# The second attention of a two-layer decoder: values as the stationary operand in two column halves, the weights divided ahead of their transposes, the mask added by transfers

## The chip, the cores and the metric

The kernel runs on one core of a Trainium2 chip. The core has five engines that each work through an instruction stream of their own: TensorE (PE, matmuls and transposes), VectorE (DVE), ScalarE (ACT), GpSimd (POOL, which here adds a few tiles and issues transfers) and SyncE (SP, which issues most transfers). The metric is the time of one execution on the device in microseconds. The kernel before was run three times: 976.5, 976.67 and 976.83 us, median 976.67.

## The reference, cut to what matters

One sequence of 256 tokens with 1024 features goes through two layers. The first has a differential attention, the second a forgetting attention whose keys, values and forget gates are computed once, between the layers. Only the second attention is changed:

```
def forgetting_attention(h, w_q, w_o, k, v, F):
    q = (h @ w_q).reshape(b, s, B_HEADS, HEAD_DIM)     # 16 heads of 64
    def block(args):                                   # 2 blocks of 128 queries
        causal = q_pos[:, None] >= k_pos[None, :]
        decay = jnp.transpose(Fqb, (0, 2, 1))[..., None] - F_k[:, :, None, :]
        logits = jnp.einsum('bqhd,bkhd->bhqk', qb, k) * scale + decay
        logits = jnp.where(causal, logits, -jnp.inf)
        p = jax.nn.softmax(logits, axis=-1)
        return jnp.einsum('bhqk,bkhd->bqhd', p, v)
    ...
    return o.reshape(b, s, B_WIDTH) @ w_o
```

Around it stand four SwiGLU feed-forward blocks, the first attention, the norms and the modulation by the vector c.

## The kernel before

Everything is held transposed, features on partitions and tokens along the rows, so that 128 features by 256 tokens is one tile. Projections are made of f32 products split in three: a weight piece `raw` is cast to a short part `wh` by ScalarE, VectorE computes the residue `wl`, activations are split into `HH` and `HL` in the same way, and `mm3` issues the three matmuls wh x high, wl x high, wh x low. Each of the three is a 128x128 load and a matmul that moves 256 columns (258 where two more columns carry a shift). The weights stream from HBM by SyncE's transfers through six buffers.

TensorE, ScalarE and VectorE take their instructions in the order in which the program writes them (the class `InOrder` records every call at line 99, which is why nearly all rows of the profile name that line). `InOrder` keeps an estimate of each engine's clock, and casts and residues of coming weight pieces are put into the gaps that this estimate shows (`bg`, `fill_act`, `fill_dve`). What GpSimd issues is not ordered this way; it is ordered by a scheduler as its inputs and buffers come free.

The second attention is `attention_b`. It works on eight pairs of heads, c = 0 to 7, in a pipeline of groups, t = 0 to 10. Between two groups a number of fill steps run on TensorE (`fills`): first the rest of the q projection (tiles `lq`), then the output projection of the finished pairs (`op.steps`, tiles `pw`). The tuple in the last loop gives the number of fill steps ahead of each group. A group t does four things for four pairs:

- pair t, `scores` and `exps`: two heads of 64 features stand on the two row halves of the array, and `sb` gets 128x128 logits for the first block of queries and 128x256 for the second. VectorE subtracts logits and decay and takes the minimum (tile `d`, `nm`), ScalarE exponentiates in place and sums the rows (`sm`). `d` holds 384 columns a head: 128 for the first block, 256 for the second; queries stand on partitions.
- pair t-1, `weights_t` and `weights_out`: three 128x128 transposes a head through the identity in the constants' tile `tri`, into the banks `wa` and `wb`, copied to `wta` by ScalarE and to `wtb` by VectorE.
- pair t-2, `values` and `divide`: three matmuls a head, the transposed weights stationary (128x128), 64 columns of `vb` moving; the result, queries on partitions, lies in the second half of `wb`. VectorE then multiplies it by the reciprocal of the row sums (`rsb`, `onb`).
- pair t-3, `out_t` and `out_split`: two transposes of `onb` into free columns of the score banks `sb`, so that features stand on partitions again; ScalarE casts to `obh`, VectorE computes the residue `obl`, as the output projection needs them.

At the end of a group `masked(t+1)` adds the causal mask on VectorE to the two diagonal 128x128 blocks of each head's `d`, and `decay(t+2)` loads the next decays: one transfer for each head, issued by GpSimd at line 1236 from a small DRAM tile `fdram` that is repeated on all partitions. `d` has six buffers, three pairs; a load therefore waits for the transposes of the pair three before it.

Of the kernel before, what the change touches and what calls it, by code (L numbers as in the profile page):

```python
# [10 lines left out]
F32 = mybir.dt.float32  # L11
# [3 lines left out]
ALU = mybir.AluOpType  # L15
PSUM = bass.MemoryType.PSUM

P = 128
# [3 lines left out]
HD = 64  # L22
# [81 lines left out]
def trunk(ctx, tc, a, out):  # L104
    nc = tc.nc
    InOrder.ready = {}
    pe = InOrder(tc, nc.tensor, 0.0, 1 / 2350)
    act = InOrder(tc, nc.scalar, 0.13, 1 / 1200)
    dve = InOrder(tc, nc.vector, 0.08, 1 / 960)
# [11 lines left out]
    def sbank(name):  # L121
        return pp.tile([P, 512], F32, tag="s", name=name, bufs=2)
# [7 lines left out]
    mm = pe.matmul  # L130
# [776 lines left out]
    for k in range(0, NC, 2):  # L907
# [3 lines left out]
        if k % 4:  # L911
            i = k // 4
# [309 lines left out]
    def attention_b():  # L1222
# [9 lines left out]
        def decay(c):  # L1232

            for hd in (2 * c, 2 * c + 1):
                d = cp_.tile([P, 384], F32, tag=DT[hd % 6], name=f"d{hd}")
                nc.gpsimd.dma_start(d, bass.AP(fdram.tensor, fdram.offset + hd * (P + S), [[0, P], [1, P + S]]))
                ds[hd] = d

        def masked(c):

            m2 = mask.rearrange("p (o k) -> p o k", o=1).to_broadcast([P, 2, P])
            for m in range(2):
                diag = ds[2 * c + m].rearrange("p (b k) -> p b k", k=P)[:, ::2]
                dve.tensor_tensor(diag, diag, m2, op=ALU.add)

        r = late_pairs("wq", q[:2], None, AF.Exp)
        for c in range(2):
# [15 lines left out]
        def exps(c, sb):  # L1263
# [10 lines left out]
                                   bias=nm[:, cc:cc + 1], scale=-1.0, accum_out=sm[:, cc:cc + 1])  # L1274
            sms[c] = sm

        def weights_t(c, ta, tb):
            for j in range(6):
                d, b = ds[2 * c + j // 3], j % 3
                pe.transpose(ta[:, j * P:j * P + P] if j < 4 else tb[:, (j - 4) * P:(j - 3) * P],  # L1280
                             d[:, b * P:b * P + P], ident)

        def weights_out(c, ta, tb):
            w0 = cp_.tile([P, 512], F32, tag="hidh8", name=f"wta{c}")
            w1 = cp_.tile([P, 256], F32, tag="hidh9", name=f"wtb{c}")
            act.copy(w0, ta)
            dve.tensor_copy(w1, tb[:, :256])
            st[c] = [w0[:, j * P:j * P + P] for j in range(4)] + [w1[:, j * P:j * P + P] for j in range(2)]

        def values(c, po):  # L1290

            for m in range(2):
                hd = 2 * c + m
                wt = st[c][3 * m:3 * m + 3]
                vs = slice((hd % 8) * HD, (hd % 8) * HD + HD)
                v0, v1 = vb[0][hd // 8][:, vs], vb[1][hd // 8][:, vs]
                mm(po[:, m * HD:m * HD + HD], wt[0], v0, start=True, stop=True)
                mm(po[:, P + m * HD:P + m * HD + HD], wt[1], v0, start=True, stop=False)
                mm(po[:, P + m * HD:P + m * HD + HD], wt[2], v1, start=False, stop=True)

        def divide(c, po):
            rs = kp.tile([P, 4], F32, tag="rs", name=f"rsb{c}")
            dve.reciprocal(rs, sms[c])
            on = kp.tile([P, 256], F32, tag="w512b", name=f"onb{c}")
            dve.tensor_tensor(on.rearrange("p (g d) -> p g d", g=4), po.rearrange("p (g d) -> p g d", g=4),
                              rs.rearrange("p (g o) -> p g o", o=1).to_broadcast([P, 4, HD]), op=ALU.mult)
            st[c] = on

        def out_t(c, pz):
            for qt in range(2):  # L1310
                pe.transpose(pz[qt], st[c][:, qt * P:qt * P + P], ident)

        def out_split(c, pz):
            oh, ol = o[c]
            for qt in range(2):
                act.copy(oh[:, qt * P:qt * P + P], pz[qt])
            for qt in range(2):
                qs = slice(qt * P, qt * P + P)
                dve.tensor_tensor(ol[:, qs], pz[qt], oh[:, qs].bitcast(F32), op=ALU.subtract)

        def group(t):

            cs, cw, cv, co = (c if 0 <= c < NP else None for c in (t, t - 1, t - 2, t - 3))
            sb = [sbank(f"sb{t}_{m}") for m in range(2)] if cs is not None or co is not None else None
            ta = abank(f"wa{t}") if cw is not None else None
            tb = bbank(f"wb{t}") if cw is not None or cv is not None else None
            if co is not None:
                pz = [sb[m][:, 384:] for m in range(2)]
                out_t(co, pz)
            if cs is not None:  # L1330
                scores(cs, sb)
            if cv is not None:
                values(cv, tb[:, 256:])
            if cw is not None:
                weights_t(cw, ta, tb)
            if co is not None:
                out_split(co, pz)
            if cs is not None:
                exps(cs, sb)
            if cv is not None:  # L1340
                divide(cv, tb[:, 256:])
            if cw is not None:
                weights_out(cw, ta, tb)
            if t + 1 < NP:
                masked(t + 1)
            if t + 2 < NP:
                decay(t + 2)

# [6 lines left out]
                for _ in op.steps():  # L1355
                    yield

        masked(0)
        fill = fills()
        for t, n in enumerate((3, 9, 7, 7, 7, 7, 7, 7, 7, 6, 5)):  # L1360
            for _ in range(n):
                next(fill)
            group(t)
        return op, fill

    pace[0] = PACE[5]
# [133 lines left out]
```

## Time and profile before

| What | Value |
| --- | --- |
| runs of the kernel, median of 3 | 976.67 us |
| span of the profiled execution, first to last instruction | 974.4 us |
| the runs' median above that span | 2.27 us |
| moved from HBM, on average over the span | 274 GB/s |
| second attention, first scores to last output transposes | 728.8 to 778.5 us of the span |
| granted TensorE clock, mean | 0.999 |

The profile is one execution. The page gives its span and no second figure for the whole execution, so what lies around the span is known only as the difference to the runs' median. Times in the views are microseconds from the span's start. TensorE appears as two rows of records, matmuls (PE) and loads of the stationary operand (PEld); an f32 matmul is recorded as two passes, each with a load of its own. Matmuls are pipelined, so their lengths overlap, and what one costs is read from the distance between starts.

### The profile page before, as it was taken

The page shows a single profiled execution, that of the slowest core. Times are in us where ns is not written, and L with a number is a line of the kernel's source. Part 1 is how long each engine was busy: PE and PEld are TensorE (multiplying, and loading weights), DVE is VectorE, ACT ScalarE, POOL GpSimd, SP SyncE. Part 2 cuts the span into 40 slices and gives each one's busy share as a digit, 9 for nine tenths or more (in the row PEclk, how much of TensorE's full clock was granted, in tenths as well). Part 3 has the DMA queues.
Part 4 walks back from the last instruction along what each step waited for, and adds up shares of the span by engine and source line. Part 5 has one row for each costly group of instructions (what it writes and reads, how often), then busy time and mean ns, then how long its engine had stood idle before and what let it go on. Part 6 is the DMA issues. An engine that isn't in the chain of part 4 may idle for free.

```text
span 974.4 us, 20491 instructions
## 1 busy us (share of the span) xinstructions
PE 963.7 (99%) x8124; PEld 939.9 (96%) x8124; DVE 818.5 (84%) x1372; ACT 552.4 (57%) x902; POOL 54.6 (6%) x94
## 2 busy tenths in 40 slices
PE   8999999999999999999999999999999999999997
PEld 6999999998999999999997999999998999999997
DVE  7989979989999999878899989989977699555575
ACT  5466545566787645455576554445567576455432
POOL 0000200000112000000000000000011014300000
PEclk9999999999999999999999999999999999999999
DMA  9988999967776699888959899998885337978651
GB/s 360 415 352 279 332 372 339 345 225 272 293 239 232 209 381 370 293 287 314 329 179 370 308 338 337 345 314 319 297 278 174 104 109 228 266 149 276 185 152 44
DMA packets 69473, 268.22 MB, mean 275 GB/s; under 512 B 9417, under 2 KB 10225, under 8 KB 59266
## 3 DMA queue, kind: packets, MB, share of 16 engines
q1 hardware_dynamic: 66016, 259.69, 76.1%
q0 software_dynamic: 3072, 6.92, 2.5%
q8 instruction: 63, 1.03, 0.4%
q10 hardware_dynamic: 290, 0.32, 0.1%
q14 instruction: 32, 0.26, 0.1%
HBM read 264.75 MB, written 2.66 MB: 274 GB/s over the span
## 4 chain that ended last, share of the span: by engine, by line
PE 97%; DVE 1%; DMA 1%; ACT 0%; issue 0%; SPq 0%; DVEq 0%; ACTq 0%
PE po L99 25%; PE pg L99 21%; PE pu L99 21%; PE pf L99 5%; PE pv L99 5%; PE pw L99 4%; PE lp L99 4%; PE pqk L99 3%; PE wb L99 1%; PE lq L99 1%; PE lu L99 1%; PE lg L99 1%; PE pk L99 1%; PE sb L99 1%; DMA ada<-in_ada 1%; PE s L99 1%
## 5 line engine op out<-in xcount | busy, mean ns | idle before, releaser
L99 ACT CAST wh<-raw 128x1024 fp32r<-128x1024 f32 (+1 forms) x360 | 347.3, 975 | 210.8 <-PE pu L99 82.0
L99 DVE TENSOR_TENSOR wl<-raw,wh 128x1024 fp32r<-128x1024 f32 (+1 forms) x360 | 398.6, 1126 | 70.9 <-ACT sg L99 20.3
L99 DVE CUSTOM_DVE_ANT_0 ada<-ada,cact,vecs 128x1024 f32<-128x1024 f32 x160 | 203.6, 1279 | 0.4 <-DMA ada<-in_ada 0.4
L99 PE MATMUL pg<-HH,wh 128*128 128x256 f32 x608 | 168.0, 276 | 0.0
L99 PE MATMUL pg<-HH,wl 128*128 128x256 f32 x608 | 167.9, 276 | 0.0
L99 PE MATMUL pu<-HH,wh 128*128 128x256 f32 x608 | 167.9, 276 | 0.0
L99 PE MATMUL pu<-HL,wh 128*128 128x256 f32 x608 | 167.9, 276 | 0.0
L99 PE MATMUL pg<-HL,wh 128*128 128x256 f32 x608 | 167.9, 276 | 0.0
L99 PE MATMUL pu<-HH,wl 128*128 128x256 f32 x608 | 167.9, 276 | 0.0
L99 PE MATMUL po<-hidh,wh 128*128 128x256 f32 x528 | 145.7, 276 | 0.0
L99 PE MATMUL po<-hidh,wl 128*128 128x256 f32 x528 | 145.7, 276 | 0.0
L99 PE MATMUL po<-hidl,wh 128*128 128x256 f32 x528 | 145.7, 276 | 0.0
L99 PEld LDWEIGHTS pg<-HH,wh 128*128 128x128 f32 x608 | 114.1, 188 | 0.7 <-issue 0.6
L99 PEld LDWEIGHTS pg<-HH,wl 128*128 128x128 f32 x608 | 114.1, 188 | 0.0
L99 PEld LDWEIGHTS pu<-HH,wh 128*128 128x128 f32 x608 | 114.1, 188 | 0.0
L99 PEld LDWEIGHTS pg<-HL,wh 128*128 128x128 f32 x608 | 114.1, 188 | 0.0
L99 PEld LDWEIGHTS pu<-HL,wh 128*128 128x128 f32 x608 | 114.1, 188 | 0.0
L99 PEld LDWEIGHTS pu<-HH,wl 128*128 128x128 f32 x608 | 114.1, 188 | 0.0
L99 PEld LDWEIGHTS po<-hidh,wh 128*128 128x128 f32 x528 | 99.1, 188 | 0.0
L99 PEld LDWEIGHTS po<-hidl,wh 128*128 128x128 f32 x528 | 99.1, 188 | 0.0
L99 PEld LDWEIGHTS po<-hidh,wl 128*128 128x128 f32 x528 | 99.1, 188 | 0.0
L99 ACT CAST hidh<-hf 128x512 fp32r<-128x512 f32 x44 | 27.3, 621 | 40.5 <-DVE hf L99 40.4
(226 smaller groups left out, 1848.4 us busy)
## 6 DMA issues: line engine op xcount, KB each, us to landing
raw<-in_win SPq DMA_DIRECT2D x176, 512.0 KB, 6.8
ada<-in_ada SPq DMA_DIRECT2D x79, 1024.0 KB, 7.2
raw<-in_wout SPq DMA_DIRECT2D x48, 384.0 KB, 5.3
raw<-in_wout SPq DMA_DIRECT2D x48, 320.0 KB, 5.5
raw<-in_wqk SPq DMA_DIRECT2D x16, 512.0 KB, 5.8
raw<-in_wo SPq DMA_DIRECT2D x16, 512.0 KB, 5.8
raw<-in_wlast SPq DMA_DIRECT2D x16, 512.0 KB, 4.5
raw<-in_wv SPq DMA_DIRECT2D x8, 512.0 KB, 7.2
```

Of the source, the lines that this page charges most:

```text
L99: return self.tc.keep_in_program_order(f(*args, **kw))
```

## The change

Four things change in `attention_b`, and nothing outside it. In `values` the 64 columns of v of one head become the stationary operand and the transposed weights move, 256 columns for the first 128 keys (both blocks of queries) and 128 for the second; the two heads of a pair write partitions 0 to 63 and 64 to 127 of one bank, which puts them on two column halves of the array. The result has features on partitions, so `out_t` is gone, and with it a stage of the pipeline: ten groups instead of eleven. The weights of a head must then lie side by side, so `weights_t` orders its six blocks anew. The division can no longer follow the values; `scale` divides `d` itself, ahead of the transposes, two fill steps before the group. The mask is no longer added by VectorE: each decay load is followed by a second transfer of GpSimd that adds the mask to the two diagonal blocks. `out_split` becomes one cast and one residue of 256 columns. The numbers of fill steps are changed to suit, and the last four run after the last group.

```diff
--- before.py
+++ after.py
@@ -1235,13 +1235,10 @@
                 d = cp_.tile([P, 384], F32, tag=DT[hd % 6], name=f"d{hd}")
                 nc.gpsimd.dma_start(d, bass.AP(fdram.tensor, fdram.offset + hd * (P + S), [[0, P], [1, P + S]]))
                 ds[hd] = d
-
-        def masked(c):
-
             m2 = mask.rearrange("p (o k) -> p o k", o=1).to_broadcast([P, 2, P])
-            for m in range(2):
-                diag = ds[2 * c + m].rearrange("p (b k) -> p b k", k=P)[:, ::2]
-                dve.tensor_tensor(diag, diag, m2, op=ALU.add)
+            for hd in (2 * c, 2 * c + 1):
+                diag = ds[hd].rearrange("p (b k) -> p b k", k=P)[:, ::2]
+                nc.gpsimd.dma_start(diag, m2, accum_op=ALU.add)
 
         r = late_pairs("wq", q[:2], None, AF.Exp)
         for c in range(2):
@@ -1274,75 +1271,58 @@
                                    bias=nm[:, cc:cc + 1], scale=-1.0, accum_out=sm[:, cc:cc + 1])
             sms[c] = sm
 
+        def scale(c):
+
+            rs = kp.tile([P, 4], F32, tag="rs", name=f"rsb{c}")
+            dve.reciprocal(rs, sms[c])
+            for m in range(2):
+                d = ds[2 * c + m]
+                for qt, (c0, w) in enumerate(QT):
+                    dve.tensor_scalar(d[:, c0:c0 + w], d[:, c0:c0 + w], rs[:, 2 * qt + m:2 * qt + m + 1], None,
+                                      op0=ALU.mult)
+
         def weights_t(c, ta, tb):
-            for j in range(6):
-                d, b = ds[2 * c + j // 3], j % 3
-                pe.transpose(ta[:, j * P:j * P + P] if j < 4 else tb[:, (j - 4) * P:(j - 3) * P],
-                             d[:, b * P:b * P + P], ident)
+            for m, b, to, i in ((0, 0, ta, 0), (0, 1, ta, 1), (0, 2, ta, 2), (1, 2, ta, 3), (1, 0, tb, 0), (1, 1, tb, 1)):
+                pe.transpose(to[:, i * P:i * P + P], ds[2 * c + m][:, b * P:b * P + P], ident)
 
         def weights_out(c, ta, tb):
             w0 = cp_.tile([P, 512], F32, tag="hidh8", name=f"wta{c}")
             w1 = cp_.tile([P, 256], F32, tag="hidh9", name=f"wtb{c}")
             act.copy(w0, ta)
             dve.tensor_copy(w1, tb[:, :256])
-            st[c] = [w0[:, j * P:j * P + P] for j in range(4)] + [w1[:, j * P:j * P + P] for j in range(2)]
+            st[c] = ((w0[:, :2 * P], w0[:, 2 * P:3 * P]), (w1, w0[:, 3 * P:]))
 
         def values(c, po):
 
-            for m in range(2):
-                hd = 2 * c + m
-                wt = st[c][3 * m:3 * m + 3]
-                vs = slice((hd % 8) * HD, (hd % 8) * HD + HD)
-                v0, v1 = vb[0][hd // 8][:, vs], vb[1][hd // 8][:, vs]
-                mm(po[:, m * HD:m * HD + HD], wt[0], v0, start=True, stop=True)
-                mm(po[:, P + m * HD:P + m * HD + HD], wt[1], v0, start=True, stop=False)
-                mm(po[:, P + m * HD:P + m * HD + HD], wt[2], v1, start=False, stop=True)
-
-        def divide(c, po):
-            rs = kp.tile([P, 4], F32, tag="rs", name=f"rsb{c}")
-            dve.reciprocal(rs, sms[c])
-            on = kp.tile([P, 256], F32, tag="w512b", name=f"onb{c}")
-            dve.tensor_tensor(on.rearrange("p (g d) -> p g d", g=4), po.rearrange("p (g d) -> p g d", g=4),
-                              rs.rearrange("p (g o) -> p g o", o=1).to_broadcast([P, 4, HD]), op=ALU.mult)
-            st[c] = on
-
-        def out_t(c, pz):
-            for qt in range(2):
-                pe.transpose(pz[qt], st[c][:, qt * P:qt * P + P], ident)
-
-        def out_split(c, pz):
+            for kt in range(2):
+                for m in range(2):
+                    hd = 2 * c + m
+                    v = vb[kt][hd // 8][:, (hd % 8) * HD:(hd % 8) * HD + HD]
+                    mm(po[m * HD:m * HD + HD, kt * P:], v, st[c][m][kt], start=kt == 0, stop=kt == 1)
+
+        def out_split(c, po):
             oh, ol = o[c]
-            for qt in range(2):
-                act.copy(oh[:, qt * P:qt * P + P], pz[qt])
-            for qt in range(2):
-                qs = slice(qt * P, qt * P + P)
-                dve.tensor_tensor(ol[:, qs], pz[qt], oh[:, qs].bitcast(F32), op=ALU.subtract)
+            act.copy(oh, po)
+            dve.tensor_tensor(ol, po, oh.bitcast(F32), op=ALU.subtract)
 
         def group(t):
 
-            cs, cw, cv, co = (c if 0 <= c < NP else None for c in (t, t - 1, t - 2, t - 3))
-            sb = [sbank(f"sb{t}_{m}") for m in range(2)] if cs is not None or co is not None else None
+            cs, cw, cv = (c if 0 <= c < NP else None for c in (t, t - 1, t - 2))
+            sb = [sbank(f"sb{t}_{m}") for m in range(2)] if cs is not None else None
             ta = abank(f"wa{t}") if cw is not None else None
             tb = bbank(f"wb{t}") if cw is not None or cv is not None else None
-            if co is not None:
-                pz = [sb[m][:, 384:] for m in range(2)]
-                out_t(co, pz)
             if cs is not None:
                 scores(cs, sb)
             if cv is not None:
                 values(cv, tb[:, 256:])
             if cw is not None:
                 weights_t(cw, ta, tb)
-            if co is not None:
-                out_split(co, pz)
             if cs is not None:
                 exps(cs, sb)
             if cv is not None:
-                divide(cv, tb[:, 256:])
+                out_split(cv, tb[:, 256:])
             if cw is not None:
                 weights_out(cw, ta, tb)
-            if t + 1 < NP:
-                masked(t + 1)
             if t + 2 < NP:
                 decay(t + 2)
 
@@ -1355,12 +1335,15 @@
                 for _ in op.steps():
                     yield
 
-        masked(0)
         fill = fills()
-        for t, n in enumerate((3, 9, 7, 7, 7, 7, 7, 7, 7, 6, 5)):
-            for _ in range(n):
+        for t, n in enumerate((3, 9, 8, 8, 8, 8, 7, 7, 6, 4)):
+            for i in range(n):
+                if 1 <= t <= NP and i == n - 2:
+                    scale(t - 1)
                 next(fill)
             group(t)
+        for _ in range(4):
+            next(fill)
         return op, fill
 
     pace[0] = PACE[5]
```

The next rows are TensorE's order in one group of the middle of the attention (sb are the score banks, wa and wb the banks of transposed weights, wb also that of the values). Before:

```order
L99 MATMUL sb_0_9700<-tri,onb_9654 128x128
L99 MATMUL sb_1_9701<-tri,onb_9654 128x128
L99 MATMUL sb_0_9700<-kT,q_9238 128x128
L99 MATMUL sb_1_9701<-kT,q_9238 128x128
L99 MATMUL sb_0_9700<-kT,q_9238 128x256
L99 MATMUL sb_1_9701<-kT,q_9238 128x256
L99 MATMUL wb_9703<-vb,wta_9656 128x64 x4
L99 MATMUL wb_9703<-vb,wtb_9657 128x64 x2
L99 MATMUL wa_9702<-tri,d_9503 128x128 x3
L99 MATMUL wa_9702<-tri,d_9505 128x128
L99 MATMUL wb_9703<-tri,d_9505 128x128 x2
```

and now:

```order
L99 MATMUL sb_0_9721<-kT,q_9238 128x128
L99 MATMUL sb_1_9722<-kT,q_9238 128x128
L99 MATMUL sb_0_9721<-kT,q_9238 128x256
L99 MATMUL sb_1_9722<-kT,q_9238 128x256
L99 MATMUL wb_9724<-wta_9668,vb 64x256
L99 MATMUL wb_9724<-wtb_9669,vb 64x256
L99 MATMUL wb_9724<-wta_9668,vb 64x128 x2
L99 MATMUL wa_9723<-tri,d_9509 128x128 x3
L99 MATMUL wa_9723<-tri,d_9511 128x128
L99 MATMUL wb_9724<-tri,d_9511 128x128 x2
```

The two output transposes at the head are gone, and six values matmuls with 64 moving columns have become four with 256 or 128, the heads in turn.

On VectorE, between the copy of one pair's transposed weights (wtb) and the subtractions for the next pair (ISA, reading sb), stood before:

```order
L99 RECIPROCAL rsb_9578<-smb_9428 128x4
L99 TENSOR_TENSOR onb_9580<-wb_9549,rsb_9578 128x256
L99 COPY wtb_9583<-wb_9549 128x256
L99 TENSOR_TENSOR d_9503<-d_9503,tri 128x2x128
L99 TENSOR_TENSOR d_9505<-d_9505,tri 128x2x128
L99 TENSOR_TENSOR wl<-raw,wh 128x1024
L99 TENSOR_TENSOR obl_9232<-sb_0_9616,obh_9228 128x128
L99 TENSOR_TENSOR obl_9232<-sb_1_9617,obh_9228 128x128
L99 ISA d_9503,nmb_9642<-sb_0_9616,d_9503 128x128
```

and now:

```order
L99 TENSOR_TENSOR wl<-raw,wh 128x1024
L99 TENSOR_TENSOR obl_9232<-wb_9559,obh_9228 128x256
L99 COPY wtb_9591<-wb_9559 128x256
L99 TENSOR_TENSOR wl<-raw,wh 128x1024
L99 RECIPROCAL rsb_9626<-smb_9575 128x4
L99 TENSOR_SCALAR d_9439<-d_9439,rsb_9626 128x128
L99 TENSOR_SCALAR d_9439<-d_9439,rsb_9626 128x256
L99 TENSOR_SCALAR d_9441<-d_9441,rsb_9626 128x128
L99 TENSOR_SCALAR d_9441<-d_9441,rsb_9626 128x256
L99 ISA d_9509,nmb_9656<-sb_0_9638,d_9509 128x128
```

The masks and the division have left this place, and the scaling of the pair's weights stands behind the residue, the copy and a weight residue, ahead of the next pair's subtractions.

On GpSimd's queue, where before only the decay loads stood (d<-fdram, one for each head, in the order of the heads), the first pairs now have:

```order
L1236 DMA d_9391<-fdram 128x384
L1236 DMA d_9393<-fdram 128x384
L1236 DMA d_9397<-fdram 128x384
L1236 DMA d_9399<-fdram 128x384
L1241 DMA d_9391<-tri 128x2x128
L1241 DMA d_9393<-tri 128x2x128
L1236 DMA d_9439<-fdram 128x384
L1241 DMA d_9397<-tri 128x2x128
L1241 DMA d_9399<-tri 128x2x128
L1236 DMA d_9441<-fdram 128x384
L1241 DMA d_9439<-tri 128x2x128
L1241 DMA d_9441<-tri 128x2x128
```

The adding transfers (d<-tri, line 1241) stand between the loads, each behind the load of the same buffer, which it waits for; a load written behind them waits in the queue as well.

## The prediction

> **What bounds the kernel now.** I read the head of the page first, then its chain of work that ended last, then what TensorE waits for, and last the stretch of the second attention by itself.
>
> ```profile
> span 974.4 us, 20491 instructions
> PE 963.7 (99%) x8124; PEld 939.9 (96%) x8124; DVE 818.5 (84%) x1372; ACT 552.4 (57%) x902; POOL 54.6 (6%) x94
> ...
> PE 97%; DVE 1%; DMA 1%; ACT 0%; issue 0%; SPq 0%; DVEq 0%; ACTq 0%
> ```
>
> TensorE (PE) is 97% of the chain that sets the end. A busy TensorE could still be a waiting one, so the list of its waits over the whole span comes next, and with it the stretch from the first to the last attention group.
>
> ```profile
> PE pf L99 <- ACT HH L99: 1.9, 1, 1.9
> PE warm L99 <- DVE one L99: 1.2, 1, 1.2
> PE pw L99 <- DVE nl L99: 0.8, 2, 0.4
> PE pf L99 <- DVE wl L99: 0.2, 1, 0.2
> ...
> 727.00:779.00 52.00, 52.00 (x448) 48.09 (x447) 37.14 (x133) 34.10 (x109) 5.32 (x10) 1.00 0.45 142
> ```
>
> These four waits sum to 4.1 us; none is in the second attention (pf and warm belong to the start, pw<-nl to the first attention). In the stretch, the columns are PE, PE's loads, DVE, ACT, POOL, clock, DMA share, GB/s: TensorE 52 of 52 us at full clock, VectorE 37.1, ScalarE 34.1, transfers at 0.45. So here a microsecond of TensorE work is a microsecond of kernel, and the others have room.
>
> **What a group costs on TensorE.** One group, by the timeline of TensorE (start, length, tiles, shape, count; f32 matmuls have two records, one for each pass):
>
> ```profile
> 753.57 0.28 PE L99 MATMUL pw<-obh,wl 128*128 128x256 f32 x1
> 753.68 0.28 PE L99 MATMUL pw<-obl,wh 128*128 128x256 f32 x1
> 753.80 0.38 PE L99 MATMUL sb<-tri,onb 128*128 128x128 f32 x2
> 754.11 0.93 PE L99 MATMUL sb<-kT,q 64*128 64x128 f32 x8
> 754.97 1.10 PE L99 MATMUL wb<-vb,wta 128*128 128x64 f32 x8
> 755.91 0.61 PE L99 MATMUL wb<-vb,wtb 128*128 128x64 f32 x4
> 756.35 0.61 PE L99 MATMUL wa<-tri,d 128*128 128x128 f32 x4
> 756.80 0.38 PE L99 MATMUL wb<-tri,d 128*128 128x128 f32 x2
> 756.94 0.36 PE L99 MATMUL pw<-obh,wh 128*128 128x256 f32 x1
> ...
> L99 PE MATMUL sb<-kT,q x64: 272/374/378, 728.8 to 766.1; 64*128 64x128 f32 x32, 64*128 64x256 f32 x32
> ```
>
> Starts count, since lengths overlap. The output transposes (onb) take 753.80 to 754.11, the scores 0.86 us, the values (vb) 754.97 to 756.35 or 1.38 us for 12 passes. A values pass moves only 64 columns but comes every 0.11 to 0.12 us: as long as a pass of 128 transposed columns (wa, 0.45 us for 4), so its 128x128 load is what it pays. The last row gives the speed of moving: the scores' passes last 272 ns at 128 columns and 378 at 256, so 128 f32 columns stream in about 0.106 us and 256 in 0.21. The scores are, for each head, 128 and 256 columns in two passes: 0.64 us a head, 1.28 for two heads after one another. They take 0.86. The two heads stand on two row halves of the array, and the row shows these running at the same time: 0.64 of streaming and 0.22 for entering and leaving the split array.
>
> **The change, part by part.**
>
> *Output transposes, gone.* 16 transposes (8 pairs of two). The nearest place without them is the first group, and one without scores is a late group:
>
> ```profile
> 728.61 0.28 PE L99 MATMUL lq<-HL,wh 128*128 128x258 f32 x1
> 728.82 0.93 PE L99 MATMUL sb<-kT,q 64*128 64x128 f32 x8
> 729.68 0.39 PE L99 MATMUL lq<-HH,wh 128*128 128x258 f32 x1
> ...
> 770.89 0.38 PE L99 MATMUL sb<-tri,onb 128*128 128x128 f32 x2
> 771.11 1.00 PE L99 MATMUL wb<-vb,wta 128*128 128x64 f32 x8
> ...
> 772.39 0.61 PE L99 MATMUL wa<-tri,d 128*128 128x128 f32 x4
> ```
>
> From the last full-array matmul to the scores it is 0.21 us without them and 0.43 with them (753.68 to 754.11): 0.22 a pair; in the late group also 0.22 (770.89 to 771.11). Eight pairs: **1.76 us**.
>
> *Values, turned round.* Now 4 matmuls a pair instead of 6; 64 columns of v are stationary, the weights move: 256 and 128 columns for each head, two passes, the heads on two column halves. Column halves are nowhere in this trace. The streaming is exactly that of the scores, so from below it is 0.64 us (halves side by side, free entry and exit), from above 1.28 plus 0.22, 1.50 (one after the other). I take the scores' 0.86, as the nearest row: same moving sizes, same head pairs, half an array each. Then 1.38 becomes 0.86 in the six groups that have scores just ahead, less about 0.04 for the first transposes' load behind a split array: 6 x 0.48 = 2.88. In the last two groups the old block is 1.28 (771.11 to 772.39); the new one has an entry of its own, 0.21 less an ordinary step of 0.12, so 0.95: 2 x 0.33 = 0.66. Together **3.54 us**.
>
> [...]
>
> *VectorE and ScalarE.* From the groups of the stretch and from the first attention, which has the scaling:
>
> ```profile
> L99 DVE TENSOR_TENSOR wl<-raw,wh 128x1024 fp32r<-128x1024 f32 x9 | 11.0, 1219 | 0.2 <-PE pw L99 0.2
> ...
> L99 DVE TENSOR_TENSOR d<-d,tri 128x256 f32<-128x256 f32 x16 | 6.0, 418 | 0.0
> L99 DVE TENSOR_TENSOR obl<-sb,obh 128x128 fp32r<-128x128 f32 x14 | 3.4, 286 | 7.2 <-ACT obh L99 7.2
> L99 DVE TENSOR_TENSOR onb<-wb,rsb 128x256 f32<-128x256 f32 x8 | 3.4, 425 | 3.4 <-PE wb L99 3.4
> L99 DVE COPY wtb<-wb 128x256 f32<-128x256 f32 x8 | 3.3, 415 | 0.0
> ...
> L99 DVE TENSOR_SCALAR nl<-nl,rs x16: 286/317/351, 222.0 to 287.1; 128x128 f32<-128x128 f32 x8, 128x256 f32<-128x256 f32 x8
> ```
>
> VectorE loses 16 x 0.418 of masks, 8 x 0.425 of division and 16 x 0.286 of residues (14.7 us), and gains 16 x (0.286 + 0.351) of scaling and 8 residues of 256 columns at about 0.42 (13.6 us). Even, 36 us in a stretch of about 47. ScalarE's two casts of a pair become one. None of it is on the path; the cover is TensorE's streaming, and it goes only if the order makes TensorE wait, as follows.
>
> *A new wait: the transposes on the scaling.* Counted from the start of a pair's scores (728.82), VectorE's part of its exponentials starts 1.0 later (first row below) and takes up to 4 x 0.35; ScalarE's ends near 3.2 (four of 0.45, second row). Then come, on VectorE, the residue (0.42), the wtb copy (0.42) and a weight residue (1.22), to 4.4 or so, and the scaling of 2 x 0.64, over near 5.7. The next group's transposes come one period (5.0 us, below) plus scores and values (1.7) later: 6.7. Slack 1.0; I take nothing, and up to 0.3 in a group or two where two weight residues stand ahead. Behind the scaling on VectorE stand the next pair's exponentials, behind the transposes on TensorE the output projection.
>
> *The masks by transfer.* POOL issues them in order: a pair's two decay loads, then, once these have landed, two adding transfers.
>
> ```profile
> L99 DVE CUSTOM_DVE_ANT_0 d<-sb,d x32: 281/356/420, 729.8 to 767.9; 128x128 f32<-128x128 f32 x16, 128x256 f32<-128x256 f32 x16
> ...
> L99 ACT ACTIVATE d<-d,nmb x32: 386/452/503, 730.1 to 768.8; 128x128 f32<-128x128 f32 x16, 128x256 f32<-128x256 f32 x16
> ...
> 748.49 0.93 PE L99 MATMUL sb<-kT,q 64*128 64x128 f32 x8
> ...
> 759.81 0.93 PE L99 MATMUL sb<-kT,q 64*128 64x128 f32 x8
> ...
> 765.50 0.93 PE L99 MATMUL sb<-kT,q 64*128 64x128 f32 x8
> ...
> 711.52 1.90 POOL L1236 DMA_DIRECT2D d<-fdram  x3 [185.25 <-PE po L99]
> ...
> 751.76 1.06 POOL L1236 DMA_DIRECT2D d<-fdram  x2 [4.69 <-ACT d L99]
> ...
> DMA to landing us min/median/max: 3.2/3.6/9.7
> ...
> DMA to landing us min/median/max: 2.1/6.4/8.2
> ...
> 814.00:839.00 25.00, 25.00 (x223) 25.00 (x222) 19.41 (x22) 13.32 (x15) 18.39 (x32) 1.00 0.95 265
> ```
>
> A period is 5.69 us (759.81 to 765.50), then about 5.0. The load for the pair two groups ahead goes out 3.3 us behind the scores (748.49 to 751.76), then about 2.8. To that pair's exponentials are left 2 x 5.0 - 2.8 + 1.0 = 8.2 us, for a load of 3.6 (d<-fdram, first landing row) and an adding transfer. The trace has none that adds; the bounds are 2.1 and 8.2 (second landing row: x<-turned, the only transfer from SBUF to SBUF, at a DMA share of 0.95 by the last row). I take 3.6 to 4, as the loads of this very stretch: no wait up to 4.6, and with the 1.0 of slack nothing lost on TensorE up to 5.6. At 8.2, 2.6 us are lost in each round of three groups (a load waits for the transposes of the pair three before it), and there are two rounds: 5.2 in all. The first pair has more time: with both transfers at their longest, 711.5 + 9.7 + 8.2 is 729.4, just ahead of its exponentials at 729.8.
>
> **The sum.** 1.76 + 3.54 = 5.3 us off TensorE's stream; the span becomes 974.4 - 5.3 = 969.1. The runs' median, 976.67, is 2.27 above the profiled span, and what lies around the span doesn't change: **971.4 us**. After the attention TensorE again waits for nothing, so what is saved stays saved.
>
> **The rivals.**
> 1. *Halves overlap in part.* Loads of one half not hidden behind the other's stream, or a head's two passes kept together so that only every other pass has company. A load in the open costs up to 0.10: the eight wta passes take 0.94 behind the scores and 0.84 (771.11 to 771.95) behind full-array work. Three more of them at 0.05 to 0.10 in 8 pairs: 1.2 to 2.4 us; passes kept together: 0.21 x 8 = 1.7. That is 972.6 to 973.8. Against it: the scores overlap fully in the same form. [...] The trace speaks against it for the whole array: full-array steps of 0.11 to 0.12 (753.57, 753.68) leave no room for a load in the open.
> 2. *The change doesn't do what it says: the column halves run one after the other.* The block grows by 0.64 x 8 = 5.1 us: 976.5, no change. For it: two streams over all 128 rows at once, which the row halves of the scores never need.
> 3. *The adding transfers come late,* 5.6 to 8.2 us: 971.4 to 976.6. For it: 6.4 is the median of x<-turned. Against: transfers are at 0.45 here.
> [...]
>
> **How the numbers follow.** Forecast 60% (its own range 969.6, entry and exit free in all 8 pairs, to 972.4); rival 1 15%, rival 2 13%, rival 3 7%, rival 4 5%. The range 969.6 to 976.5 takes in both ends of the unknown block. 0.2% is 1.95 us, about what a measurement of this kernel can tell from no change: faster is under 974.7, which holds the forecast, rival 1 and most of rival 3 (0.81); rival 2 and the rest of 3 are the same (0.14); rival 4 is slower (0.05).
>
> **What would show it.** [...] A wait of TensorE's wa for VectorE's d, or of VectorE's d<-sb for a transfer, shows the two new waits, and the landing time of d<-tri decides rival 3. The prediction is wrong if the values block isn't like the scores block, or if the saved time reappears as a wait of TensorE behind the attention.

## The result, and the profile after

| Kernel | median of the runs, us | lowest to highest | profiled run: time, span |
| --- | --- | --- | --- |
| before (6 runs beside the changed ones) | 976.75 | 976.50 to 981.08 | 976.67 (median of the first three), 974.4 |
| changed (6 runs) | 983.43 | 981.03 to 988.69 | 983.71, 981.7 |

The changed kernel is slower: ratio 1.0068, interval 1.0044 to 1.0092. Forecast were 971.4 us and a range up to 976.5. Runs of one kernel, of the one before too, scatter upwards by some 4 us or more (its cause, as far as one is seen, is in the last section), so single runs are not compared, and the stretches of a trace are.

The head of the changed kernel's page and its chain of work that ended last, as quoted of before:

```profile
span 981.7 us, 20425 instructions
PE 962.2 (98%) x8076; PEld 933.6 (95%) x8076; DVE 820.0 (84%) x1372; ACT 552.2 (56%) x894; POOL 74.5 (8%) x110
...
PE 91%; DVE 3%; issue 3%; DMA 1%; POOL 1%; ACT 1%; DVEq 0%; POOLq 0%; ACTq 0%
```

TensorE has less to do (962.2 us busy against 963.7) and is 91% of the chain, not 97%: what came instead is waiting. The waits of TensorE and, from the list of VectorE, the one for a transfer (in total, times, longest):

```profile
PE wb L99 <- DVE rsb L99: 3.3, 2, 2.4
PE pw L99 <- DVE lt L99: 1.8, 1, 1.8
PE wa L99 <- DVE d L99: 1.4, 2, 0.9
PE wb L99 <- DVE wtb L99: 1.3, 2, 0.9
PE sb L99 <- DVE nmb L99: 0.8, 1, 0.8
```

```profile
DVE d L99 <- DMA d<-tri: 7.1, 4, 2.9
```

All eight waits lie in the second attention, which had none before: 8.6 us. The rows of TensorE name five tiles of VectorE, and it would be easy to look for the fault there. VectorE's own list gives the source: its part of the exponentials, the subtraction that writes d, waited four times, 7.1 us in all, for the adding transfers (d<-tri). The list puts three more waits of this subtraction (2.2, 0.8 and 0.5 us) down to TensorE, but like the four they end 0.16 us behind the landing of an adding transfer: 10.6 us in all, in every pair from the fourth on. In this trace each adding transfer that came late made VectorE late, and TensorE then met whichever of VectorE's tiles it needed next.

TensorE's timeline (start, length, tiles, shape, count), at an undisturbed group and at the longest wait:

```profile
737.45 0.93 PE L99 MATMUL sb<-kT,q 64*128 64x128 f32 x8
738.30 0.43 PE L99 MATMUL wb<-wta,vb 128*64 128x256 f32 x1
738.31 0.43 PE L99 MATMUL wb<-wtb,vb 128*64 128x256 f32 x1
738.57 0.38 PE L99 MATMUL wb<-wta,vb 128*64 128x256 f32 x1
738.58 0.38 PE L99 MATMUL wb<-wtb,vb 128*64 128x256 f32 x1
738.78 0.39 PE L99 MATMUL wb<-wta,vb 128*64 128x128 f32 x4
739.10 0.66 PE L99 MATMUL wa<-tri,d 128*128 128x128 f32 x4
...
739.73 0.37 PE L99 MATMUL lq<-HH,wh 128*128 128x258 f32 x1
...
775.93 0.28 PE L99 MATMUL pw<-obl,wh 128*128 128x256 f32 x1
778.58 0.45 PE L99 MATMUL wb<-wta,vb 128*64 128x256 f32 x1 [2.37 <-DVE rsb L99]
...
779.89 1.12 PE L99 MATMUL wa<-tri,d 128*128 128x128 f32 x4
...
781.08 0.56 PE L99 MATMUL pw<-obh,wh 128*128 128x256 f32 x1
```

The values block is what the forecast said it would be: passes of the two heads start 0.01 us apart, and from the first to the transposes it is 0.80 us (738.30 to 739.10; forecast 0.86, old block 1.38). The saving is there; it was spent on waiting. Behind the wait of 2.4 us the same block takes 1.31 us (778.58 to 779.89) and the six transposes 1.19 (779.89 to 781.08) where they take 0.63 (739.10 to 739.73). Windows of the changed kernel show why (busy time of PE, PE's loads, DVE, ACT, POOL, then granted clock, DMA share, GB/s):

```profile
748.00:758.00 10.00, 7.89 (x68) 6.29 (x68) 7.06 (x23) 6.23 (x18) 7.00 (x8) 1.00 0.58 111
...
768.00:778.00 10.00, 6.56 (x54) 5.41 (x52) 5.15 (x21) 5.34 (x17) 2.46 (x2) 1.00 0.47 93
778.00:788.00 10.00, 9.42 (x69) 8.50 (x70) 5.84 (x15) 5.47 (x10) 0.00 (x0) 0.83 0.36 109
```

The granted clock falls to 0.83 in the window behind the wait. Compared with the undisturbed group, the values block and the transposes lose about 1.1 us there.

Now GpSimd, which issues the loads (L1236) and the adding transfers (L1241). Its timeline in the changed kernel, brackets: idle before, and for whom:

```profile
741.35 2.14 POOL L1236 DMA_DIRECT2D d<-fdram  x2
748.08 2.46 POOL L1241 DMA_DIRECT2D d<-tri  x2 [4.58 <-DMA d<-fdram]
750.05 1.66 POOL L1236 DMA_DIRECT2D d<-fdram  x2
754.62 2.46 POOL L1241 DMA_DIRECT2D d<-tri  x2 [2.92 <-DMA d<-fdram]
756.11 2.14 POOL L1236 DMA_DIRECT2D d<-fdram  x2
762.87 1.23 POOL L1241 DMA_DIRECT2D d<-tri  x1 [4.61 <-DMA d<-fdram]
...
765.26 1.62 POOL L1236 DMA_DIRECT2D d<-fdram  x2
```

and the view of line 1241 by itself (instructions, idle time before them, landing):

```profile
L1241 POOL DMA_DIRECT2D d<-tri x16: 1172/1228/1723, 716.1 to 771.5; - x16
...
  DMA d<-fdram: 31.3, 11
...
DMA to landing us min/median/max: 3.0/5.4/9.3
```

From one pair's loads to the next pair's is 8.70 us (741.35 to 750.05), 6.06 (750.05 to 756.11) and 9.15 (756.11 to 765.26), though the attention wants a pair about every 5. In each round the queue stands still until the loads have landed (31.3 us in all) and issues two adding transfers, 1.2 us each; only then does it reach the next pair's loads. Their buffers had been free for 4 to 6 us by then: the transposes that free them were followed by TensorE's next work at 745.10, 752.48 and 759.21, and the loads went out at 750.05, 756.11 and 765.26. Three theories follow from this, and the runs below set them apart.

- **A, the order in the queue.** The next loads stand behind adding transfers that wait: a chain of load, landing, add, load that is longer than a group.
- **B, the adding transfers themselves.** They take time of the DMA engines, of the SBUF or of GpSimd's issuing; or (**B'**) load and adding transfer in a row are longer than the 8.2 us that three pairs of buffers leave, whatever the queue.
- **C, the scaling.** Not the masks but the new wait of the transposes on the scaled weights sets the end.

### The profile page after: what moved, and what is told of

Same layout as the page of the kernel before. It is cut to its first block, busy times and chain, and to the rows that moved or that the text cites. A ratio compares the mean times of both kernels' runs of the same rounds, so it can differ in the third digit from the quotient of the medians.

```text
span 981.7 us, 20425 instructions
## 1 busy us (share of the span) xinstructions
PE 962.2 (98%) x8076; PEld 933.6 (95%) x8076; DVE 820.0 (84%) x1372; ACT 552.2 (56%) x894; POOL 74.5 (8%) x110
## 4 chain that ended last, share of the span: by engine, by line
PE 91%; DVE 3%; issue 3%; DMA 1%; POOL 1%; ACT 1%; DVEq 0%; POOLq 0%; ACTq 0%
PE po L99 25%; PE pg L99 21%; PE pu L99 21%; PE pf L99 5%; PE pv L99 5%; PE lp L99 4%; PE pqk L99 3%; PE pw L99 2%; PE pk L99 1%; DVE wl L99 1%; DMA d<-tri 1%; PE lq L99 1%; DVE HL L99 1%; PE s L99 1%; PE lu L99 1%
```

## The experiments

Ratios are to the kernel before, run on the same chip; the experiments ran on three chips, so a difference of two medians is rough. Diffs are against the changed kernel unless the text says otherwise.

**The masks back on VectorE**, all else as changed.

```diff
-                nc.gpsimd.dma_start(diag, m2, accum_op=ALU.add)
+        def masked(c):
...
+                dve.tensor_tensor(diag, diag, m2, op=ALU.add)
```

> The changed kernel with the masks added by VectorE again, where they stood before; values in column halves, scaling ahead of the transposes and all else as changed. Theory A (the loss is the round trip in GpSimd's queue: the loads of a pair stand behind the adding transfers of the pair before, which wait for their own loads to land, about 7 us a pair against a period of 5): 970.5 to 972.5 us, TensorE waits for nothing in the second attention. Theory B (adding transfers are costly in themselves, by their traffic or their issue): the same, 970.5 to 972.5. Theory C (the loss is the new wait of the transposes for the scaling, and the masks only coincide with it): over 976.

Measured 972.09 us (971.77 to 976.53, 11 runs), ratio 0.9944 (0.9924 to 0.9965). The only wait of TensorE in the attention, from its list:

```profile
PE pw L99 <- DVE lt L99: 0.6, 1, 0.6
```

C falls: the transposes never wait for the scaling. The terms for transposes and values come out at the forecast's 971.4 within a microsecond, and the transfers alone cost 983.43 - 972.09 = 11.3 us. The traces agree: from the first scores to the last matmul of the output projection it is 58.0 us in the kernel before (728.8 to 786.8), 64.6 in the changed one (728.9 to 793.5) and 53.2 here (728.7 to 781.9), so the saving is 4.8 us of the 5.3 forecast and the loss 11.4. This version beats both kernels.

**The kernel before, with the adding transfers alone** (diff against before).

```diff
-        def masked(c):
...
-                dve.tensor_tensor(diag, diag, m2, op=ALU.add)
+                nc.gpsimd.dma_start(diag, m2, accum_op=ALU.add)
```

> The kernel before with the one edit that the masks are added by transfers; values, division and groups as before. A: a round of about 7 us a pair against a period of 5.7, so over some six pairs 4 to 9 us slower than before, 980 to 986. B: slower too, by 2 us or more. C: no change, 976 to 977.5.

Measured 983.39 us (981.84 to 989.09, 10 runs), ratio 1.0049 (1.0027 to 1.0071). The transfers harm the old kernel as well, by about half as much: the stretch of the attention is 63.5 us in its trace (729.7 to 793.2), 5.5 more than before. Why half was not tested; its period is longer, 5.7 us. In its list of waits they show up under yet another name, the old kernel's output transposes waiting for the divided values:

```profile
PE sb L99 <- DVE onb L99: 3.1, 2, 1.8
```

**The loads issued by SyncE**, the adding transfers alone on GpSimd.

```diff
-                nc.gpsimd.dma_start(d, bass.AP(fdram.tensor, ...
+                sp.dma_start(d, bass.AP(fdram.tensor, ...
```

> The changed kernel with the decay loads issued by SyncE, so that on GpSimd's queue only the adding transfers stand and no load waits behind them. A: most of the loss goes, 971 to 975. B: the adding transfers stay as slow, 979 or more. C: 980 or more.

Measured 983.77 us (982.5 to 988.3, 10 runs), ratio 1.0055 (1.0032 to 1.0078): a miss for A as it was put. The trace shows that the run asked another question. From SyncE's view of the tile d up to 760 us, and from TensorE's waits:

```profile
L99 SPq DMA_DIRECT2D d<-fdram x12: 319/364/432, 726.9 to 753.3; - x12
```

```profile
PE sb L99 <- DVE nmb L99: 4.6, 1, 4.6
PE pw L99 <- DVE lt L99: 2.9, 1, 2.9
```

SyncE reached the first loads only at 726.9 us, behind its weight pieces, where GpSimd issued them at 711.6; the first pair was late, and the largest wait, 4.6 us, comes from that. The wait of 2.9 us (lt) comes later, at 758, and where it comes from stays open. The run says nothing for or against A.

**Masks on VectorE, and plain transfers of the adding ones' shape into tiles that nobody reads** (diff against the version with the masks on VectorE).

```diff
+                nc.gpsimd.dma_start(spare.rearrange("p (b k) -> p b k", k=P), m2)
```

> Masks on VectorE as in the first run, and beside them GpSimd issues plain transfers of the same shape from the same mask into spare tiles that nobody reads: the traffic and the issue without the wait for the loads and without the adding. A: as the first run, within 1 us of it. B, if it is traffic or issue: 2 us or more above the first run. C: as the first run, whatever that is.

Measured 982.06 us (980.33 to 986.34, 10 runs), ratio 1.0037 (1.0017 to 1.0057). Again the order had shifted: nothing ties these transfers to their pair, and GpSimd's scheduler put all sixteen ahead of the later loads. There is a single wait in the attention:

```profile
PE wa L99 <- DVE d L99: 9.4, 1, 9.4
```

A miss as a test of traffic; as a test of the queue it shows what transfers ahead of a load in GpSimd's queue cost, even if no one needs them. So the same was run in the program's order:

```diff
+                tc.keep_in_program_order(nc.gpsimd.dma_start(spare.rearrange("p (b k) -> p b k", k=P), m2))
```

> The fourth run again with GpSimd's queue in program order (there all spare transfers were moved ahead of the loads and held them up once): masks on VectorE, and behind each pair's two loads two plain transfers of the mask's shape into spare tiles. A and B': as with the masks on VectorE alone, 971.5 to 973. B by traffic or issue: 976 or more.

Measured 972.74 us (971.98 to 973.66, 5 runs), ratio 0.9949 (0.9931 to 0.9966), against 972.09 without the transfers. In this kernel's timeline of GpSimd two plain transfers take 1.42 us to issue:

```profile
736.79 1.42 POOL L1241 DMA_DIRECT2D spare<-tri  x2
```

By these medians the plain transfers' bytes and issuing cost 0.65 us, and TensorE's one wait in this attention is the 0.6 us for lt that the version without them has too. As a stand-in for adding ones they are not complete: the bytes are the same, the packets are not, as GpSimd's queue shows (packets, MB, share of the DMA engines), here and, second, in the changed kernel:

```profile
q0 software_dynamic: 3840, 9.02, 3.2%
```

```profile
q0 software_dynamic: 7424, 9.02, 4.1%
```

With the masks on VectorE the queue has 3072 packets, so the plain transfers make 768 and the adding ones 4352. For bytes B falls here; for packets and for the adding itself it is settled only by the runs below that keep the adding transfers.

**The adding transfers one group behind their loads:** eight buffers, loads three groups ahead, and in the queue, kept in the program's order, the loads of pair t+3 before the adding transfers of pair t+2, which by then find their loads landed.

```diff
+            if t + 3 < NP:
+                decay(t + 3)
             if t + 2 < NP:
-                decay(t + 2)
+                added(t + 2)
```

> The changed kernel with eight buffers for the decays instead of six, the loads three groups ahead, and GpSimd's queue in program order with a pair's adding transfers one group behind its loads: load of pair t+3, then adding for pair t+2. So no adding transfer waits for a fresh load, and each has some 8 us until its use. A (queue order) and B' (load and adding one after the other are longer than the 8 us window): 971 to 974. B (adding transfers cost in themselves): 978 or more.

Measured 975.28 us (971.83 to 983.19, 10 runs), ratio 0.9988 (0.9962 to 1.0014). The profiled run was the lowest, 971.83; in its attention TensorE waits only 0.7 us for lt, and the stretch from the first scores to the last matmul of the output projection is 52.9 us. So the order and the buffers can remove the whole loss, with all sixteen adding transfers in place; the median lies above because six of the ten runs took 974 to 983, and no profile of such a run was taken.

**Loads from the third pair on by ScalarE:** only the queue changes, not the buffers.

```diff
-                nc.gpsimd.dma_start(d, bass.AP(fdram.tensor, ...
+                (act if c >= 2 else nc.gpsimd).dma_start(d, src)
```

> The changed kernel with the decay loads from the third pair on issued by ScalarE at the end of a group, three pairs of buffers as changed, the adding transfers alone on GpSimd's queue. A: no load stands behind an adding transfer, most of the loss goes: 971.5 to 975. B': load (4 to 5 us), issue (1.2 each) and adding (4 to 5) still make 10 to 11 us for a window of 8: 976 to 982.

Measured 977.62 us (976.71 to 983.36, 10 runs), ratio 1.0003 (0.9985 to 1.002). With the loads out of GpSimd's queue, 5.8 of the 11.3 us are gone; 5.5 stay, as B' had it. From VectorE's list:

```profile
DVE d L99 <- issue: 2.5, 2, 1.9
DVE d L99 <- PE wb L99: 2.0, 2, 1.6
```

The list doesn't name the adding transfers, but each of these four waits ends 0.12 us behind the landing of one. The fifth pair shows why: its loads went out from 743.04 on, and its adding transfers landed at 754.08 and 755.37, 11 to 12 us later, against a window of about 8.

**Eight buffers, loads three groups ahead, but the queue as changed** (load, load, add, add of the same pair, here kept in the program's order from the first pair on).

```diff
-            if t + 2 < NP:
-                decay(t + 2)
+            if t + 3 < NP:
+                decay(t + 3)
```

> The changed kernel with eight buffers and the loads three groups ahead, but the queue as changed: load, load, adding, adding, pair by pair. The window grows from 8 to 13 us. A: a round stays at about 7 us a pair, so the queue falls behind all the same after the first pairs: 975 to 981. B': 971 to 974.

Measured 984.69 us (983.11 to 987.89, 4 runs), ratio 1.0074 (1.0045 to 1.0103): no gain, and more than A expected. GpSimd's timeline in this kernel:

```profile
735.79 1.62 POOL L1236 DMA_DIRECT2D d<-fdram  x2
740.78 2.46 POOL L1241 DMA_DIRECT2D d<-tri  x2 [3.37 <-DMA d<-fdram]
742.27 2.13 POOL L1236 DMA_DIRECT2D d<-fdram  x2
748.09 1.23 POOL L1241 DMA_DIRECT2D d<-tri  x1 [3.69 <-DMA d<-fdram]
```

The round is 6.48 us (735.79 to 742.27) with buffers to spare. A queue that delivers a pair every 6 to 8 us falls behind a consumer of one every 5. The longer window alone did not help while the order stayed (984.69 us, six buffers 983.43). What the program's order by itself does to the first pairs was not run, so this version is not compared with the changed one to the microsecond.

**ScalarE's loads and the eight buffers together,** the loads on ScalarE from the fourth pair on.

> The changed kernel with the decay loads from the fourth pair on issued by ScalarE, so that GpSimd's queue holds adding transfers only, and with eight decay buffers instead of six, loads three groups ahead instead of two. With ScalarE's loads alone (six buffers) 977.6 us were measured, about 5 above the version with the masks on VectorE (972.1). If those 5 us are the window (a load and an adding transfer in a row are longer than the about 8 us that six buffers leave), a window one group longer takes them away: 971.5 to 974, and VectorE waits for no transfer in the attention. If the adding transfers cost something besides being late, it stays at 976 to 979. If loads on ScalarE hold ScalarE up (a load stands in its queue until the transposes free the buffer), TensorE waits for ScalarE's tiles and it is above 978.

Measured 973.2 us (972.23 to 977.44, 10 runs), ratio 0.9963 (0.9952 to 0.9975). TensorE's list has no wait in the attention, and VectorE none for a transfer. Yet the adding transfers, by the view of their line in this kernel, are no faster than in the changed one:

```profile
L1242 POOL DMA_DIRECT2D d<-tri x16: 1173/1194/1709, 718.4 to 758.2; - x16
...
DMA to landing us min/median/max: 3.0/6.5/9.7
```

They land in a median of 6.5 us and cost about nothing: 1.1 us over the version with the masks on VectorE, within what the two intervals leave open. With that B falls for packets and for the adding too. The loss had two steps, and only both cures together remove it: the order in the queue (983.43 to 977.62) and the window (977.62 to 973.2). Neither does it alone: the longer window without the other queue gave 984.69. The stretch from the first scores to the last matmul of the output projection, which leaves out the rest of the program, says the same: 64.6 us in the changed kernel, 57.1 with ScalarE's loads, 66.1 with the eight buffers, 52.8 with both, 53.2 with the masks on VectorE.

**The values head by head**, on the version with the masks on VectorE: to see whether side-by-side halves hang on the alternating order in which `values` writes them.

```diff
-            for kt in range(2):
-                for m in range(2):
+            for m in range(2):
+                for kt in range(2):
```

> The version with the masks on VectorE (972.1 us), but with the values' four matmuls of a pair ordered head by head (first both key blocks of one head, on one column half, then both of the other) instead of alternating. If the two column halves run side by side only where neighbouring matmuls are on different halves, only the middle pass of the eight has company: the values block grows from 0.80 us to between 1.3 and 1.5, and the time by 8 x 0.5 to 0.7, to 976 to 977.7. If the order doesn't matter (each half takes its matmuls from a queue of its own), the block stays at 0.8 and the time at 972.

Measured 972.0 us (971.63 to 972.15, 4 runs), ratio 0.9943 (0.9926 to 0.9959). TensorE's timeline in this kernel:

```profile
738.62 0.43 PE L99 MATMUL wb<-wta,vb 128*64 128x256 f32 x1
738.63 0.43 PE L99 MATMUL wb<-wtb,vb 128*64 128x256 f32 x1
738.89 0.38 PE L99 MATMUL wb<-wta,vb 128*64 128x256 f32 x1
738.90 0.38 PE L99 MATMUL wb<-wtb,vb 128*64 128x256 f32 x1
739.10 0.40 PE L99 MATMUL wb<-wta,vb 128*64 128x128 f32 x4
739.43 0.44 PE L99 MATMUL wa<-tri,d 128*128 128x128 f32 x2
```

The program now writes both matmuls of the first head (256 and 128 columns) before the second head's (wtb, 256). In the trace wtb starts 0.01 us behind wta all the same, and the block is 0.81 us. The order made no difference: 972.0 us against 972.09.

**The fill steps moved**, one from ahead of the fourth group to ahead of the seventh, on the same version.

> The version with the masks on VectorE (972.1 us), but with one fill step fewer ahead of the fourth group and one more ahead of the seventh. Its only wait of TensorE in the attention is 0.6 us for a weight residue (lt) in the fourth stretch of fill steps, where VectorE is late; if that wait only hangs on how many fill steps stand ahead, it goes and the time is 971.5. If VectorE is behind there whatever the fill steps, it stays or moves: 972 to 972.5. Either is near what the measurement can tell.

Measured 974.48 us (971.99 to 978.72, 10 runs), ratio 0.9969 (0.9951 to 0.9987); the row of the wait is unchanged, 0.6 us for lt. Moving one fill step doesn't touch it. Nothing gained; the median over 972 can't be told from scatter.

## Why the prediction was wrong

- **Output transposes and values (1.76 and 3.54 us): right.** With the masks left on VectorE the time is 972.09, where the sum gave 971.4, and the attention is 4.8 us shorter in the traces, where it gave 5.3. The block measured 0.80 us against the 0.86 borrowed from the scores. The way to that number, to look in the same trace for an instruction of the same shape on half an array, held.
- **Rivals 1, 2 and 4: fell.** The two halves ran side by side (passes 0.01 us apart), the loads of the second and third passes start 0.21 us ahead of their matmuls (738.36 and 738.57 against 738.57 and 738.78, in the trace of the changed kernel), and the block is 0.80 us for 0.64 of streaming. Even with a head's passes kept together, the condition of rival 1, it is 0.81 us (head by head, 972.0). Rival 4, the 5% on a slower kernel, was the author's estimate, and no run shows its price. The kernel did come out slower, but not by this block, which is 0.58 us shorter than the old one.
- **The transposes on the scaling (slack 1.0, taken as nothing): right as long as the masks are on time.** With masks on VectorE there is no such wait. In the changed kernel it shows in two places (wa<-d, 1.4 us), as a consequence of the late masks.
- **VectorE and ScalarE off the path: right**, in the same sense, but for 0.6 us that TensorE waits for a weight residue (lt).
- **The masks by transfer: the step that failed.** It was put as "POOL issues them in order: a pair's two decay loads, then, once these have landed, two adding transfers", and then each pair was priced by its own window alone: 8.2 us, less a load, less an adding transfer, "no wait up to 4.6". The sentence has what was needed, and the pricing left it out: whatever waited in GpSimd's queue delayed what stood behind it (31.3 us of waits in the changed kernel, the loads 4 to 6 us after their buffers were free), and behind a pair's adding transfers stand the next pair's loads. The window assumed that a load goes out when its buffer is free. In the changed kernel it goes out when the pair ahead has been added to, and the round, 6.06 to 9.15 us above, is longer than the period of 5. Each pair inherits the delay of the pair ahead, which a window counted for one pair can't show. The runs put 5.8 us on this (loads by ScalarE) and 4.4 on the window that remained too short.
- **The sizes in that step were low, too.** Loads were priced at 3.6 us, the median of before, and landed in a median of 5.9; in the rounds above the adding transfers go out 6.7 us (741.35 to 748.08) and 4.6 us (750.05 to 754.62) behind their loads. The adding transfer was taken at 3.6 to 4 and landed in a median of 5.4 (a plain one of the same bytes in 5.1, so the adding is not what makes it long); issuing two takes 2.46 us, a term that the sum didn't have. By these numbers the window alone would have been overrun.
- **Rival 3 had the mechanism and too low a price.** "The adding transfers come late" is what happened; its dearest case was 5.2 us lost, and it was 11.3. It counted two rounds of 2.6 us, no queue, and nothing for what late work sets off: the waits of 8.6 us less the 0.6 that the version with VectorE's masks has too, and a stretch at the lower clock (0.83, about 1.1 us). These leave some 2 us of the 11.3 that are not itemized; the list counts a wait as short (the longest as 2.37, where the distance between starts is 2.65 and an ordinary step 0.11).

The order in the queue was in reach before the run: the prediction's own sentence has the adding transfers held back until their loads have landed. The trace of the changed kernel has the price: GpSimd stood still for 31.3 us in 11 such waits. What would happen without them no run here shows. The question left out was who else needs the engine that is made to wait.

## What to carry to other kernels

When dependent transfers are put on one in-order queue, price the round and not the pair: time to land, plus issuing, plus the next wait, against the period at which the consumer takes them; more buffers didn't help a round that was longer than the period (984.69 us with eight, a round of 6.48 us against a period of 5). Put the dependent transfer behind the next pair's load (971.83 us in the profiled run, 975.28 in the median), or on a queue of its own, and start it early enough (973.2); or leave the work on an engine that has room, as VectorE had here (972.09). And when an engine's list of waits names five different tiles at once, look in the other engine's list for the one wait that they share, and compare its ends with the landings of the transfers, since the list can name another cause.

## What the hardware showed that was not expected

- **Matmuls on two column halves ran out of the program's order.** Written head by head, the second head's first matmul started 0.01 us behind the first head's first, ahead of the first head's second. (The trace has start times alone; that TensorE was given the matmuls head by head is known from the source, which keeps every call of TensorE in the program's order.) Both halves use all 128 rows (128*64 in the rows), and the block is 0.80 us with the heads in turn and 0.81 head by head, for 0.64 of streaming; that figure is an estimate from the scores' passes (272 ns at 128 columns, 378 at 256).
- **TensorE's clock was lower behind a wait of 2.4 us.** It was granted 0.83 in the 10 us behind it, against 1.00 before; the distance between the starts around the wait is 2.65 us. The wait of 1.8 us (lt, a distance of 2.09) left the clock at 1.00 in the window that holds its end, 748 to 758. But in the kernel before with the adding transfers alone a distance of 2.05 us (773.12 to 775.16) was followed by a clock of 0.50 from 777 to 780 us, so in these two traces the length of the wait doesn't decide by itself.
- **An adding transfer costs GpSimd more to issue than a plain one of the same bytes:** 1.2 us against 0.71. It also makes more packets, 272 against 48 each; whether these set the price was not tested.
- **TensorE had a slightly longer step in one run, and the granted clock doesn't show it.** The profiled run with the masks on VectorE took 975.72 us, 3.6 over its median; the head-by-head run 972.15. Windows of the two in the last feed-forward block, the first row of each, in that order:

```profile
820.00:840.00 20.00, 20.00 (x172) 20.00 (x171) 11.00 (x13) 9.42 (x11) 10.43 (x18) 1.00 1.03 261
```

```profile
820.00:840.00 20.00, 20.00 (x179) 20.00 (x178) 12.21 (x14) 10.29 (x11) 9.86 (x17) 1.00 1.03 274
```

  In the same 20 us there are 172 matmuls and 179, both without a gap and at a clock of 1.00: 4% longer steps. The three windows that follow, to 900 us, have the same two counts; 80 us at 4% are 3.2 us, which is most of the difference between the two runs. The profiled runs of the kernel before and of the changed one have 179 in these windows as well, so the comparison of those two is free of it. Why it comes and goes stays open, and with it whether all of the scatter, that of the run with adding transfers a group later among it, is of this kind.
